# The end of a mixture-of-experts layer: a small expert last but one, its sums between the last one's pieces

## The chip, the cores and the metric

The kernel runs on one core of a Trainium2 chip. The metric is the time of one execution on the device in microseconds (us), as the median of several runs. The engines are TensorE (PE: matmuls), VectorE (DVE), ScalarE (ACT), GpSimd (POOL) and SyncE (SP, which here only issues DMAs). Each works through its own queue in order.

## The reference

One decoder layer on 1024 tokens of width 1024: a mixer (windowed attention and gated linear attention), then a feed-forward part in which a router picks 4 of 32 experts for each token. The change lies in the experts and the final norm:

```
u     = xb @ w_mlp1[e] + b_mlp1[e]                # 1024 -> 2048, even columns gate, odd ones linear
x_glu = jnp.minimum(u[..., ::2], 7.0)
x_lin = jnp.clip(u[..., 1::2], -7.0, 7.0)
a     = x_glu * sigmoid(1.702 * x_glu) * (x_lin + 1)
y     = a @ w_mlp2[e] + b_mlp2[e]                 # summed over a token's 4 experts with its gates
...
x = x + gt2 * rms_norm(y, g_post_ffn)             # the end of the layer, for each token
```

All is float32; the kernel makes each float32 matmul of three float16 ones (high x high, low x high, high x low).

## The kernel before, in words

Experts are ranked by their number of tokens, and rank r has room for `CAPS[r]` tokens (368 down to 60). `ORDER` is the sequence in which the ranks are computed; it alternates large and small ones. Its last four have 244, 80, 152 and 124 tokens; place 18 has 140.

An expert is done in two stages. `up` makes 8 pieces j of 128 gated columns, each from 48 matmuls into PSUM (`pu`). Behind each piece ScalarE makes `gl` (L1127) and `sg` (L1129), VectorE three instructions on `lin` (L1131 to L1133), and GpSimd the float16 pair: a cast to `aTh` (L1134) and the difference `aTl` (L1135). `down` makes the 1024 outputs from 192 matmuls into `pyv`, which ScalarE copies to `yT`. `combine` gives steps: transposes on TensorE, a scaled copy to `yo` on ScalarE (L1173) for each half of a block of 128 tokens, and after the second half an indirect DMA from GpSimd's queue that adds the rows to `yacc` in HBM (L1176).

Weights come as float32 pieces of 1 MB into 7 buffers `st` (L1059, on SP's queue). `split` turns a piece into float16 high parts on ScalarE (`eh`, L172) and low parts on VectorE (`el`, L173), two of each to a megabyte: 16 for an `up`, 8 for a `down`; their buffers hold four pieces of 512 columns ahead of TensorE, which are 16 splits.

The main loop runs `up` of expert i+1 and then `down` of expert i, so that the sequence at the end is up(29), down(28), up(30), down(29), sums of 29, down(30). Steps that are at hand (gathers of expert i+2, sums of i-1) are handed to `up` as `between` and go one by one between its pieces; what is left runs after it. Before the last expert (31, rank 19, 124 tokens) all that is left, the sums of 30, is run at once (`run(left)`).

Then comes the end. The last `up` has no `between`. The rows of `x1d` (the input of the feed-forward part) and of `yacc` (the sum) are loaded for 8 blocks of 128 tokens; each block's row is squared and summed on ScalarE (`square`, L1334), multiplied with the gate row `gfb` on VectorE (L1363), `rms` makes the factors for four blocks at a time, and VectorE scales and adds (L1368) before SP stores the block. The tokens of the last expert, whose sums are not in `yacc`, are gathered by `tokL` (L1342), finished apart (L1383 to L1390), and written over the stored rows by one last indirect DMA (L1391). A run-time loop for experts with more tokens than room follows; it has no rounds here.

The code gives each instruction a program order, and a planner, which has costs of its own, sets each engine's queue from it. `tc.issue_after(ins)` keeps what is traced inside it behind `ins` on that engine. Here the squares of blocks 0 to 3 are held behind `sgs[t - 5]`, the sigmoids of the last `up`'s pieces 3 to 6, and the others behind the activation table's load (`tail`, set 6, which stands behind the last sigmoid).

Of the kernel before, what the change touches and what calls it, by code (L numbers as in the profile page):

```python
# [9 lines left out]
F32 = mybir.dt.float32  # L10
# [3 lines left out]
AF = mybir.ActivationFunctionType  # L14
OP = mybir.AluOpType
# [5 lines left out]
D = 1024  # L21
NT = 8
# [20 lines left out]
ORDER = []  # L43
for _i in range(NE // 4):
    for _r in ((_i + 4) % 8, 15 - (_i + 4) % 8):
        ORDER += [_r, NE - 1 - _r]


@with_exitstack
def layer_kernel(  # L50
# [4 lines left out]
    nc = tc.nc  # L55
    x = x.rearrange("b s d -> (b s) d")
    out = out.rearrange("b s d -> (b s) d")
# [24 lines left out]
    x1d = dram.tile([T, D], F32, name="x1d")  # L82
    yacc = dram.tile([T + DUMP, D], F32, name="yacc")
# [338 lines left out]
    with tc.tile_pool(name="p2", bufs=1) as p2, tc.tile_pool(name="wk", bufs=2) as wk, \  # L422
# [261 lines left out]
        for t in range(NT):  # L684
            tk = slice(t * 128, (t + 1) * 128)
            row = ada_row(t // 2 - 1) if t and t % 2 == 0 else []
# [358 lines left out]
    with tc.tile_pool(name="stB", bufs=7, reuse_waits="tile") as stB, tc.tile_pool(name="sp", bufs=8, reuse_waits="tile") as sp, \  # L1045
# [50 lines left out]
        def run(steps):  # L1096
            while steps:
                steps.pop(0)()

        def up(n, w1e, bc, xT, tag, behind=(), between=(), lead=None, wp=None):  # L1100

            xTh, xTl = xT
            aTh = mo.tile([128, 8, n], F16, name="aTh", tag="aTh" + tag)
# [1 line left out]
            for j in range(8):  # L1105
# [25 lines left out]
                nc.vector.tensor_scalar(lin, pu[1], bc(1, j), bc(2, j), op0=OP.max, op1=OP.min)  # L1131
                nc.vector.scalar_tensor_tensor(lin, lin, bc(3, j), sg, op0=OP.add, op1=OP.mult)  # L1132
                lins.append(nc.vector.scalar_tensor_tensor(lin, gl, LIM * SG, lin, op0=OP.subtract, op1=OP.mult))  # L1133
                nc.gpsimd.tensor_copy(aTh[:, j, :], lin)  # L1134
                lows.append(nc.gpsimd.tensor_tensor(aTl[:, j, :], lin, aTh[:, j, :], op=OP.subtract))  # L1135
                for _ in range((len(between) + 7 - j) // (8 - j)):
                    between.pop(0)()
            return aTh, aTl
# [61 lines left out]
                gi = lambda b: tokL  # L1200
            return gather(CAPS[ORDER[i]], gi, "BS"[i % 2])

        def up_of(i, e, xT, behind=(), between=(), lead=None, wp=None):
            r = ORDER[i]

            def piece_of(j):
                if e[min(j, 1)] is None:
                    with tc.issue_after(loads[-1].ins):
                        e[1] = expert(i, perm1)
                return w1[ds(e[min(j, 1)], 1)]  # L1210

            return up(CAPS[r], piece_of,
                      lambda q, j: bt[:, q, j, r:r + 1], xT, "BS"[i % 2], behind, between, lead, wp)

# [90 lines left out]
        for i in range(NE - 1):  # L1307
# [10 lines left out]
            yTs = down(n, w2[ds(e[1], 1)], aT)  # L1318
            left = combine(n, yTs, si, gc)
            e, aT = en, aTn  # L1320
        run(left)


        i = NE - 1
        r = ORDER[i]
        n = CAPS[r]
        assert n <= 128
        aTh, aTl = up_of(i, e, xT[i][0])
        wps = [w for half in range(2) for w in pieces(w2[ds(e[1], 1)], half)]
        with tc.issue_after(sgs[-1].ins):  # L1330
            tail = act_set(6).ins

        def square(yt, ss, m):
            nc.scalar.activation(junk[:m, 0:yt.shape[-1]], yt, AF.Square, accum_out=ss)  # L1334

        gfb = mo.tile([128, D], F32, name="gfb", tag="xTlB")
        nc.sync.dma_start(gfb, bcast_row(gmod[5:6, :], D))
        junk = mo.tile([128, D], F16, name="junk", tag="xThB")

        rows = [mw.tile([128, D], F32, name=f"row{j}", tag="xg", bufs=4) for j in range(2)]  # L1340
        for row, src in zip(rows, (x1d, yacc)):
            nc.gpsimd.indirect_dma_start(out=row[:n, :], out_offset=None, in_=src,  # L1342
                                         in_offset=bass.IndirectOffsetOnAxis(ap=tokL[:n, 0:1], axis=0))
        xys = []
        for t in range(NT):
            if t < NT - 2:
                st = stB.tile([128, 4, 512], F32, name="st").rearrange("p a n -> p (a n)")
                xys.append((st[:, 0:D], st[:, D:2 * D]))
            elif t < NT - 1:
                xys.append([mw.tile([128, D], F32, name=f"xy{j}", tag="xg", bufs=4) for j in range(2)])  # L1350
            else:
                xys.append([mo.tile([128, D], F32, name=f"xy{j}", tag=f"aT{j}B") for j in "hl"])
        for xy, src, ts in ((0, x1d, range(4)), (1, yacc, range(NT)), (0, x1d, range(4, NT))):
            for t in ts:
                nc.sync.dma_start(xys[t][xy], src[t * 128:(t + 1) * 128, :])
        fs = rt.tile([128, 3, NT + 5], F32, name="fs")
        for t0 in range(0, NT, 4):
            for t in range(t0, t0 + 4):
                yt = xys[t][1]
                with tc.issue_after(sgs[t - 5].ins if t < 4 else tail):  # L1360
                    square(yt, fs[:, 0, t:t + 1], 128)
                with tc.issue_after(lins[min(t - 4, -1)].ins):
                    nc.vector.tensor_tensor(yt, yt, gfb, op=OP.mult)  # L1363
            rms(*[fs[:, j, t0:t0 + 4] for j in range(3)], 128, (tail, lins[-1].ins))
            for t in range(t0, t0 + 4):
                x1, yt = xys[t]
                with tc.issue_after(lins[-1].ins):
                    nc.vector.scalar_tensor_tensor(yt, yt, fs[:, 1, t:t + 1], x1, op0=OP.mult, op1=OP.add)  # L1368
                nc.sync.dma_start(out[t * 128:(t + 1) * 128, :], yt)
        yo = mw.tile([128, D], F32, name="yo")  # L1370
        nc.gpsimd.tensor_copy(si_l[:n], tokI[:n, r:r + 1])
        x1, yt = rows[0][:n], rows[1][:n]
        for half, pool, tag in ((0, psV, "pyv"), (1, psU, "pu")):
            py = [pool.tile([128, 512], F32, name="pyr", tag=tag)[:n, 0:256] for _ in range(2)]
            for k in range(8):
# [115 lines left out]
```

## Time and profile before

| | us |
|---|---|
| median of 3 runs (1977.88 to 1984.84) | 1979.7 |
| the profiled execution, its own time | 1985.62 |
| its span, first to last instruction | 1983.8 |
| TensorE busy in it | 1821.8 |
| VectorE busy | 1553.4 |
| ScalarE busy | 1305.1 |
| GpSimd busy | 981.2 |

Times in the views are microseconds from the start of the span; each instruction has a line of the kernel (L1334), and a tile that it writes and those that it reads (`aTh<-lin`). Matmuls are pipelined, so TensorE's busy time overstates its work.

### The profile page before, as it was taken

What the parts mean: (1) busy time and instruction counts of PE and PEld (TensorE: products, weight loads), DVE (VectorE), ACT (ScalarE), POOL (GpSimd) and SP (SyncE); (2) the same over time, 40 slices, a digit from 0 to 9 for tenths busy, and PEclk for the clock granted to TensorE, in tenths of its full rate; (3) what the DMA queues carried; (4) which work ended last, traced back from release to release, by engine and by line L of the source; (5) the groups of instructions that cost most, each with busy time, mean ns of one, the idle gap of its engine ahead of it and who ended that gap; (6) DMA issues with size and microseconds to landing.
All of it is one profiled execution on the core that took longest, in us unless ns stands there. A gap on an engine that the chain in (4) does not pass through costs nothing. (4 is left out here: it accounts for less than half of the span.)

```text
span 1983.8 us, 55399 instructions
## 1 busy us (share of the span) xinstructions
PE 1821.8 (92%) x22803; PEld 1593.0 (80%) x22803; DVE 1553.4 (78%) x2572; ACT 1305.1 (66%) x2247; POOL 981.2 (49%) x977
## 2 busy tenths in 40 slices
PE   7999999999588999999999999999989999999981
PEld 3456887755387999999999997778878888999971
DVE  6824667656679898998998996679787978989864
ACT  5623455433366878787787885668676868968762
POOL 2204777636636456555574673336443643755430
PEclk9999999989788999999999999999999999999995
DMA  8512333343499999999999997699988989999993
GB/s 280 167 44 75 91 92 98 100 140 128 137 355 321 331 353 320 353 360 329 346 346 361 371 348 268 212 316 327 323 273 292 356 275 338 365 322 327 317 314 129
DMA packets 296246, 525.79 MB, mean 265 GB/s; under 512 B 18672, under 2 KB 79227, under 8 KB 295956
## 3 DMA queue, kind: packets, MB, share of 16 engines
q1 hardware_dynamic: 277810, 476.78, 69.2%
q0 software_dynamic: 16880, 41.21, 8.7%
q8 instruction: 180, 2.95, 0.6%
q10 hardware_dynamic: 1298, 4.21, 0.5%
q14 instruction: 78, 0.64, 0.1%
HBM read 482.37 MB, written 39.76 MB: 263 GB/s over the span
## 5 line engine op out<-in xcount | busy, mean ns | idle before, releaser
L173 DVE SCALAR_TENSOR_TENSOR el<-st,eh 128x1024 f16<-128x1024 f32 x768 | 935.0, 1240 | 91.1 <-ACT eh L172 89.2
L172 ACT ACTIVATE eh<-st 128x1024 f16<-128x1024 f32 x768 | 794.0, 1055 | 237.9 <-PE pu L152 128.7
L151 PE MATMUL pu<-xTh,eh 128*128 128x232 f16 (+31 forms) x4096 | 780.4, 231 | 8.6 <-DVE lin L1131 5.0
L153 PE MATMUL pu<-xTh,el 128*128 128x232 f16 (+31 forms) x4096 | 779.6, 231 | 6.0 <-issue 6.0
L152 PE MATMUL pu<-xTl,eh 128*128 128x232 f16 (+31 forms) x4096 | 779.4, 231 | 2.9 <-issue 2.7
L152 PEld LDWEIGHTS <-eh 128*128 128x128 f16 x6080 | 595.4, 99 | 42.5 <-issue 20.4
L151 PEld LDWEIGHTS <-eh 128*128 128x128 f16 x6080 | 593.1, 98 | 30.1 <-issue 8.1
L153 PEld LDWEIGHTS <-el 128*128 128x128 f16 x6080 | 592.8, 98 | 26.2 <-issue 4.3
L1134 POOL CAST aTh<-lin 128x232 f16<-128x232 f32 (+31 forms) x256 | 298.3, 1165 | 497.3 <-DVE lin L1133 450.2
L151 PE MATMUL pyv<-aTh,eh 128*128 128x232 f16 (+30 forms) x1984 | 374.2, 231 | 9.7 <-ACT yT L1161 7.9
L153 PE MATMUL pyv<-aTh,el 128*128 128x232 f16 (+30 forms) x1984 | 373.7, 230 | 1.2 <-issue 1.2
L152 PE MATMUL pyv<-aTl,eh 128*128 128x232 f16 (+30 forms) x1984 | 373.6, 230 | 0.7 <-issue 0.7
L1135 POOL TENSOR_TENSOR aTl<-lin,aTh 128x232 f16<-128x232 f32 (+31 forms) x256 | 257.8, 1007 | 20.7
L1131 DVE TENSOR_SCALAR lin<-pu,bt 128x232 f32<-128x232 f32 (+31 forms) x256 | 109.8, 429 | 75.5 <-PE pu L153 58.0
L1176 POOL DMA_INDIRECT yacc<-yo,tokI x52 | 95.2, 1832 | 110.4 <-ACT yo L1173 103.8
L1127 ACT ACTIVATE gl<-pu,bt 128x232 f32<-128x232 f32 (+31 forms) x256 | 98.2, 384 | 69.9 <-PE pu L153 40.0
L1132 DVE SCALAR_TENSOR_TENSOR lin<-lin,bt,sg 128x232 f32<-128x232 f32 (+31 forms) x256 | 104.8, 410 | 21.0 <-ACT sg L1129 7.0
L645 POOL TENSOR_TENSOR st<-st,sil 128x512 f32<-128x512 f32 x64 | 68.7, 1074 | 92.6 <-DMA st<-in_w_ada_dram 92.2
L1129 ACT ACTIVATE sg<-gl,c 128x232 f32<-128x232 f32 (+31 forms) x256 | 108.1, 422 | 1.0
L1133 DVE SCALAR_TENSOR_TENSOR lin<-gl,lin 128x232 f32<-128x232 f32 (+31 forms) x256 | 82.9, 324 | 4.3
L1089 POOL DMA_INDIRECT xg<-h2d,gatI x50 | 71.7, 1434 | 24.4 <-PE pxh L1081 12.3
L1081 PE MATMUL pxh<-identh,xg 128*128 128x128 f16 (+27 forms) x848 | 55.7, 206 | 23.9 <-DVE xTl L1083 11.4
(408 smaller groups left out, 2495.5 us busy)
## 6 DMA issues: line engine op xcount, KB each, us to landing
st<-in_w_mlp_dram SPq DMA_DIRECT2D x384, 1024.0 KB
st<-in_w_ada_dram SPq DMA_DIRECT2D x64, 256.0 KB
xt<-in_x_dram SPq DMA_DIRECT2D x16, 512.0 KB
st<-in_w_ada_dram SPq DMA_DIRECT2D x16, 512.0 KB
st<-in_w_in_dram SPq DMA_DIRECT2D x7, 1024.0 KB
x1d<-xt SPq DMA_DIRECT2D x8, 512.0 KB
h2d<-h2s SPq DMA_DIRECT2D x8, 512.0 KB
yacc<-yi ACTq DMA_DIRECT2D x8, 512.0 KB
```

The costliest lines, as they stand in the source:

```text
L151: nc.tensor.matmul(ps, sh, mh, start=first, stop=False)
L152: nc.tensor.matmul(ps, sh, ml, start=False, stop=False)
L153: return nc.tensor.matmul(ps, sl, mh, start=False, stop=last)
L172: return (nc.scalar.activation(dh, src, AF.Copy, scale=SW), nc.vector.scalar_tensor_tensor(dl, src, SW, dh, op0=OP.mult, op1=OP.subtract))
L173: nc.vector.scalar_tensor_tensor(dl, src, SW, dh, op0=OP.mult, op1=OP.subtract))
L1127: nc.scalar.activation(gl, pu[0], AF.Relu, scale=-SG, bias=bc(0, j))
L1129: sgs.append(nc.scalar.activation(sg, gl, AF.Sigmoid, scale=-1.702 * INV / SG, bias=c7))
L1131: nc.vector.tensor_scalar(lin, pu[1], bc(1, j), bc(2, j), op0=OP.max, op1=OP.min)
L1132: nc.vector.scalar_tensor_tensor(lin, lin, bc(3, j), sg, op0=OP.add, op1=OP.mult)
L1134: nc.gpsimd.tensor_copy(aTh[:, j, :], lin)
L1135: lows.append(nc.gpsimd.tensor_tensor(aTl[:, j, :], lin, aTh[:, j, :], op=OP.subtract))
L1176: end["dma"] = nc.gpsimd.indirect_dma_start(out=yacc, out_offset=bass.IndirectOffsetOnAxis(ap=si(b)[:m, :], axis=0), in_=yo[:m, :], in_off ...
```

## The change

`ORDER` is altered in three places: rank 15 (140 tokens) goes from place 18 to place 29, rank 12 (152) from place 30 to place 18, rank 28 (80) from place 29 to place 30. The last four then have 244, 140, 80 and 124 tokens. `run(left)` ahead of the last `up` is taken out, and the sums of expert 30 (one block of 80, two steps) are handed to it as `between`. That `up` is called with `pool=False`: its casts are made by ScalarE and its differences by VectorE. Block 7 takes the place of block 1 in the sequence; blocks are taken as (0, 7, 1, 2) and (3, 4, 5, 6). Loads: all eight of `x1d`, then all eight of `yacc`, then the two gathers of the last expert's rows. Squares and gate products of blocks 0 and 7 are held behind the last but one sigmoid and the last but one gated product, those of the other six behind the last ones.

```diff
+ORDER[ORDER.index(15)], ORDER[-3], ORDER[-2] = 12, 15, 28
...
-                nc.gpsimd.tensor_copy(aTh[:, j, :], lin)
-                lows.append(nc.gpsimd.tensor_tensor(aTl[:, j, :], lin, aTh[:, j, :], op=OP.subtract))
+                if pool:
+                    nc.gpsimd.tensor_copy(aTh[:, j, :], lin)
+                else:
+                    nc.scalar.activation(aTh[:, j, :], lin, AF.Copy)
+                eng = nc.gpsimd if pool else nc.vector
+                lows.append(eng.tensor_tensor(aTl[:, j, :], lin, aTh[:, j, :], op=OP.subtract))
...
-        run(left)
...
-        aTh, aTl = up_of(i, e, xT[i][0])
+        aTh, aTl = up_of(i, e, xT[i][0], (), left, pool=False)
...
+        def rows_of(tok, m, src, **place):
+            row = mw.tile([128, D], F32, name="row", **place)
+            nc.gpsimd.indirect_dma_start(out=row[:m, :], out_offset=None, in_=src,
+                                         in_offset=bass.IndirectOffsetOnAxis(ap=tok[:m, 0:1], axis=0))
+            return row
...
-        rows = [mw.tile([128, D], F32, name=f"row{j}", tag="xg", bufs=4) for j in range(2)]
-        for row, src in zip(rows, (x1d, yacc)):
-            nc.gpsimd.indirect_dma_start(out=row[:n, :], out_offset=None, in_=src,
-                                         in_offset=bass.IndirectOffsetOnAxis(ap=tokL[:n, 0:1], axis=0))
         xys = []
         for t in range(NT):
-            if t < NT - 2:
+            if t == 0:
+                xys.append([mw.tile([128, D], F32, name=f"xy{j}", tag="xg", bufs=4) for j in range(2)])
+            elif t < NT - 1:
                 st = stB.tile([128, 4, 512], F32, name="st").rearrange("p a n -> p (a n)")
                 xys.append((st[:, 0:D], st[:, D:2 * D]))
-            elif t < NT - 1:
-                xys.append([mw.tile([128, D], F32, name=f"xy{j}", tag="xg", bufs=4) for j in range(2)])
             else:
                 xys.append([mo.tile([128, D], F32, name=f"xy{j}", tag=f"aT{j}B") for j in "hl"])
-        for xy, src, ts in ((0, x1d, range(4)), (1, yacc, range(NT)), (0, x1d, range(4, NT))):
-            for t in ts:
+        for xy, src in enumerate((x1d, yacc)):
+            for t in (0, NT - 1, *range(1, NT - 1)):
                 nc.sync.dma_start(xys[t][xy], src[t * 128:(t + 1) * 128, :])
+        x1l, ytl = [rows_of(tokL, n, src, tag="xg", bufs=4) for src in (x1d, yacc)]
         fs = rt.tile([128, 3, NT + 5], F32, name="fs")
-        for t0 in range(0, NT, 4):
-            for t in range(t0, t0 + 4):
+        for ts, pin in (((0, 7, 1, 2), -2), ((3, 4, 5, 6), -1)):
+            j0 = 4 * (pin == -1)
+            for j, t in enumerate(ts):
                 yt = xys[t][1]
-                with tc.issue_after(sgs[t - 5].ins if t < 4 else tail):
-                    square(yt, fs[:, 0, t:t + 1], 128)
-                with tc.issue_after(lins[min(t - 4, -1)].ins):
+                at = min(pin + j // 2, -1)
+                with tc.issue_after(sgs[at].ins):
+                    square(yt, fs[:, 0, j0 + j:j0 + j + 1], 128)
+                with tc.issue_after(lins[at].ins):
                     nc.vector.tensor_tensor(yt, yt, gfb, op=OP.mult)
```

## Rows read from the trace of the kernel before

**Rows 1.** The page's first part: busy time, share, instructions.
```profile
PE 1821.8 (92%) x22803; PEld 1593.0 (80%) x22803; DVE 1553.4 (78%) x2572; ACT 1305.1 (66%) x2247; POOL 981.2 (49%) x977
```

**Rows 2.** Stretches of the end: length, each engine's busy time (instructions), clock, DMA.
```profile
1902.60:1922.70 20.10, 20.10 (x370) 20.10 (x368) 15.25 (x25) 15.48 (x27) 7.80 (x11) 1.00 0.92 289
1922.70:1936.30 13.60, 5.96 (x42) 4.62 (x40) 6.23 (x13) 4.46 (x9) 5.03 (x7) 0.75 0.99 285
...
1967.90:1983.80 15.90, 0.00 (x0) 0.00 (x0) 0.00 (x0) 0.00 (x0) 1.35 (x1) 0.50 0.12 34
```

**Rows 3.** GpSimd's timeline: start, length, instruction [idle before, what ended it].
```profile
1904.50 1.40 POOL L1176 DMA_INDIRECT yacc<-yo,tokI  x1 [0.55 <-ACT yo L1173]
1913.87 1.33 POOL L1342 DMA_INDIRECT row<-yacc,tokL  x1 [7.97 <-DMA yacc<-yo,tokI]
...
1967.92 1.35 POOL L1391 DMA_INDIRECT out_dram<-row,tokL  x1 [29.84 <-SPq L1408]
```

**Rows 4.** ScalarE's timeline in the last up-projection.
```profile
1917.87 1.06 ACT L1334 ACTIVATE junk<-st 128x1024 f16<-128x1024 f32 x1 [2.59 <-DMA st<-yacc]
1918.83 0.19 ACT L1334 ACTIVATION_READ_ACCUMULATOR junk<-st 128x1 f32 x1
...
1928.24 1.06 ACT L1334 ACTIVATE junk<-st 128x1024 f16<-128x1024 f32 x1 [5.55 <-DMA st<-yacc]
...
1933.59 1.06 ACT L1334 ACTIVATE junk<-st 128x1024 f16<-128x1024 f32 x1 [3.52 <-DMA st<-yacc]
...
1934.64 0.34 ACT L1127 ACTIVATE gl<-pu,bt 128x124 f32<-128x124 f32 x1
```

**Rows 5.** VectorE's timeline in the last up-projection and at the end.
```profile
1916.04 0.41 DVE L1131 TENSOR_SCALAR lin<-pu,bt 128x124 f32<-128x124 f32 x1 [3.14 <-POOL aTl L1135]
...
1936.00 0.29 DVE L1133 SCALAR_TENSOR_TENSOR lin<-gl,lin 128x124 f32<-128x124 f32 x1
...
1954.96 1.28 DVE L1368 SCALAR_TENSOR_TENSOR xyl<-xyl,fs,xyh 128x1024 f32<-128x1024 f32 x1
```

**Rows 6.** SP's timeline: issues of loads and stores, neighbours merged (xN).
```profile
1913.60 0.80 SPq L1355 DMA_DIRECT2D st<-yacc  x2
...
1945.84 1.53 SPq L1369 DMA_DIRECT2D out_dram<-st  x2
...
1956.92 0.99 SPq L1369 DMA_DIRECT2D out_dram<-xyl  x1
```

**Rows 7.** Stretches: up(140), down(140), up(80), up(152), down(80), sums of 29; columns as above.
```profile
1324.90:1352.50 27.60, 27.60 (x439) 27.31 (x438) 21.23 (x30) 22.97 (x36) 15.06 (x14) 1.00 0.87 247
1388.80:1400.80 12.00, 12.00 (x201) 11.96 (x199) 11.69 (x18) 8.51 (x13) 9.50 (x8) 1.00 1.05 375
1806.60:1825.10 18.50, 16.77 (x429) 16.36 (x427) 17.69 (x30) 18.32 (x32) 8.86 (x11) 1.00 1.03 347
1846.50:1874.50 28.00, 28.00 (x421) 27.95 (x420) 25.14 (x36) 23.81 (x36) 15.44 (x14) 1.00 0.94 291
1874.40:1882.50 8.10, 7.25 (x197) 7.15 (x195) 8.06 (x11) 7.30 (x12) 5.75 (x5) 1.00 0.93 307
1882.50:1887.30 4.80, 1.44 (x17) 1.24 (x16) 3.67 (x4) 3.17 (x5) 1.03 (x1) 1.00 1.09 356
```

**Rows 8.** VectorE's groups from 1899 on: count, busy, mean ns, idle before.
```profile
L173 DVE SCALAR_TENSOR_TENSOR el<-st,eh 128x1024 f16<-128x1024 f32 x11 | 13.6, 1240 | 3.1 <-ACT eh L172 3.1
...
L1363 DVE TENSOR_TENSOR st<-st,gfb 128x1024 f32<-128x1024 f32 x6 | 7.3, 1219 | 0.5 <-ACT junk L1334 0.5
L1131 DVE TENSOR_SCALAR lin<-pu,bt 128x124 f32<-128x124 f32 x8 | 3.2, 402 | 10.1 <-ACT gl L1127 6.6 <-POOL aTl L1135 3.5
L1132 DVE SCALAR_TENSOR_TENSOR lin<-lin,bt,sg 128x124 f32<-128x124 f32 x8 | 2.9, 363 | 0.3
L1133 DVE SCALAR_TENSOR_TENSOR lin<-gl,lin 128x124 f32<-128x124 f32 x8 | 2.3, 283 | 0.2
```

**Rows 9.** ScalarE's timeline in the up-projection of 152 tokens.
```profile
1854.64 0.69 ACT L1173 ACTIVATE yo<-pxy,gcol 128x512 f32<-128x512 f32 x1
```

More of the change, by code (lines that the diff above doesn't have):

```diff
@@ L1098, in run, with up @@
                 steps.pop(0)()
-        def up(n, w1e, bc, xT, tag, behind=(), between=(), lead=None, wp=None):
+        def up(n, w1e, bc, xT, tag, behind=(), between=(), lead=None, wp=None, pool=True):
             xTh, xTl = xT
@@ L1201, in fetch, with up_of @@
             return gather(CAPS[ORDER[i]], gi, "BS"[i % 2])
-        def up_of(i, e, xT, behind=(), between=(), lead=None, wp=None):
+        def up_of(i, e, xT, behind=(), between=(), lead=None, wp=None, pool=True):
             r = ORDER[i]
@@ L1212, in up_of @@
             return up(CAPS[r], piece_of,
-                      lambda q, j: bt[:, q, j, r:r + 1], xT, "BS"[i % 2], behind, between, lead, wp)
+                      lambda q, j: bt[:, q, j, r:r + 1], xT, "BS"[i % 2], behind, between, lead, wp, pool)
         e = [expert(0, perm), None]
@@ L1363, in layer_kernel @@
                     nc.vector.tensor_tensor(yt, yt, gfb, op=OP.mult)
[L1364 to L1369, printed above, removed]
+            rms(*[fs[:, j, j0:j0 + 4] for j in range(3)], 128, (tail, lins[-1].ins))
@@ L1370, in layer_kernel @@
+            with tc.issue_after(lins[-1].ins):
+                for j, t in enumerate(ts):
+                    x1, yt = xys[t]
+                    nc.vector.scalar_tensor_tensor(yt, yt, fs[:, 1, j0 + j:j0 + j + 1], x1, op0=OP.mult, op1=OP.add)
+                    nc.sync.dma_start(out[t * 128:(t + 1) * 128, :], yt)
         yo = mw.tile([128, D], F32, name="yo")
         nc.gpsimd.tensor_copy(si_l[:n], tokI[:n, r:r + 1])
-        x1, yt = rows[0][:n], rows[1][:n]
+        x1, yt = x1l[:n], ytl[:n]
```

## The prediction

> **What bounds the kernel now.** I read the page first: TensorE and VectorE are both busy most of the span [rows 1], so the body is a balance, and an edit there pays only where one of them waits. Then the table of stretches of the end [rows 2]. The last expert's up-projection ends near 1922.7 us. In the next 13.6 us TensorE is busy for 5.96 us and its granted clock falls from 1.00 to 0.75 in the mean (a mix of the 2.4 and the 1.2 GHz level): something starves it while it should be doing the last down-projection.
>
> The timelines say what starves it. GpSimd issues the second sum of the last but one expert into `yacc` at 1904.50 and then the gather of `yacc` rows at 1913.87, which waited 7.97 us for that sum to land [rows 3]. It is an in-order queue: the casts and differences of the last expert (L1134, L1135) stand behind that gather, and VectorE waits 3.14 us for one of them at 1916.04 [rows 5]. ScalarE has the squares of the output rows (L1334) between the last expert's activations. They wait for rows of `yacc`, 5.55 us at 1928.24 and 3.52 us at 1933.59, and so the last `gl` comes only at 1934.64 [rows 4]. The last gated product (L1133) starts at 1936.00 and ends at 1936.29 [rows 5]: 13.6 us after TensorE had its sum ready. That is the wait that ends last in this stage, and it is on the path: from 1936.3 VectorE works with hardly a pause until the last output row is scaled at 1956.24 (19.95 us), the last output store is issued at 1956.92 [rows 6], the final scatter waits for all stores and starts at 1967.92 [rows 3], 11.0 us later, and the run ends 15.9 us after that [rows 2]. So the end of the kernel is the time of the last gated product plus 47.5 us, and the change must move that product or shorten what follows.
>
> **The change, part by part.** (a) *The order.* The sequence 244, 80, 152, 124 at the end becomes 244, 140, 80, 124, and 152 takes the place of 140 at place 18. TensorE's matmuls are the same in all; what changes is where it waits. An up-projection of 140 tokens takes 27.6 us, one of 80 takes 18.5 us (VectorE is busy for 17.69 us of it), one of 152 takes 28.0 us [rows 7]. Down-projections take 12.0 us (140) and 8.1 us (80) [rows 7]. The up-projection of the last but one therefore begins at 1846.5 + (27.6 − 18.5) = 1855.6 us, plus at place 18 0.4 us up and 0.8 us down (12.0 × 152/140 = 13.0, 1.0 more, of which I take 0.8), so 1856.8. Then 18.5 (80 up) + 12.0 (140 down) + 4.8 (sums that run at once, as before [rows 7]) + 8.1 (80 down) = 43.4: the last up-projection begins at 1900.2. It has 384 matmuls; 370 took 20.1 us [rows 2], so 20.9 us, and I allow 0.6 us for the eight transposes that now stand between its pieces: it ends at 1921.7, against 1922.7. The order itself gives 1.0 us there.
>
> VectorE can be later than that. From 1856.8 it has 40 weight differences to make (56 for the projections left, less 16 for the four pieces that the buffers hold ahead) at 1.24 us, and 16 groups of gating products at 0.40 + 0.36 + 0.28 us [rows 8]; 49.6 + 16.6 = 66.2 us, 1923.0. Both answers agree within 1.3 us.
>
> (b) *Casts and differences on ScalarE and VectorE.* This removes 8 casts and 8 differences from GpSimd and with them the 3.14 us wait. No row shows the cast on ScalarE; the nearest is `gl` of the same width, 0.34 us [rows 4], from below it is nothing if ScalarE waits anyway; I take 0.34, 8 × 0.34 = 2.7 us on ScalarE, hidden as long as it waits for rows. The difference on VectorE is nearest to L1133, 0.28 us [rows 8]: 2.3 us, which I add: 1925.3, with the price zero as the lower bound (1923.0) if the differences fall into VectorE's waits. Half of it gives 1924.2 for the last gated product without any other wait.
>
> (c) *Sums between pieces.* The sum of 80 tokens has one block, not two, and its halves come after pieces 0 and 1. In the up-projection of 152 its like did this: the second half's ScalarE copy starts at 1854.64 [rows 9], 8.1 us after the start at 1846.5, with pieces of 28.0/8 = 3.5 us. Here they are 2.7 us, so the copy is at 1900.2 + 8.1 − 1.6 = 1906.7, the sum is issued at about 1907.6, later than the 1904.50 of before. It landed 9.4 us after its issue [rows 3], which gives 1917.0, 3.5 us later than before. This is the edit's cost: SP's loads of `yacc` and GpSimd's gather both stand behind it. What was queued behind that gather on GpSimd was the casts; now nothing is. The first row of `yacc` was in use 4.3 us after its issue (1913.60 [rows 6] to 1917.87 [rows 4]), which gives 1921.3 here.
>
> The Trainium skill, in "DMA: Bandwidth & Descriptors", section "Anatomy of one DMA — SWDGE (gpsimd) path", fits one such transfer by 2.0 us plus its bytes at 436 GB/s; for 80 rows of 4 KB that is 2.8 us, an estimate from that page. The trace disagrees with its 9.4 us under load. By the page the rows would be in use at 1914.7 and the next part's 1.8 us would vanish.
>
> (d) *Squares and products at the end.* Six of eight squares no longer stand ahead of any `gl`. Those of rows 0 and 7 stand behind the seventh sigmoid and so ahead of the last `gl`: two squares and their products. With the rows at 1921.3 and, say, 1922.5, and 1.25 us each (1.06 + 0.19), the squares end at 1923.8, a cast of 0.34 us comes between, and the last `gl` starts at about 1924.2. From that start to the end of the last product it took 1.65 us before (1934.64 to 1936.29), so it ends at 1925.9, say 1926.0. That is 1.8 us later than without them, and 10.3 us ahead of 1936.3. TensorE's last down-projection then runs without the long pauses and off the path, and its clock's fall no longer matters.
>
> Behind it VectorE has six products of 1.22 us [rows 8] left where it had five: 19.95 + 1.22 = 21.2 us, to 1947.2 (bounds: 20 if the cover is better, 23.6 if none of the eight is done ahead). ScalarE's six squares, 7.5 us, run beside it. The eight loads of `x1d` now all come ahead of `yacc`, into the time before the sum lands, so less has to move afterwards: 8 rows of 0.5 MB and the gather, 4.5 MB, at the 285 GB/s of that stretch [rows 2] take 15.8 us, to about 1934 with 1 us for the last landing; VectorE reaches the second four at about 1935. So the loads are just hidden; if they are 5 us later they end last.
>
> (e) *Stores.* Before, first store to scatter was 1945.84 [rows 6] to 1967.92, 22.1 us for 4.5 MB. The first four rows now leave some 8 us ahead of the second four, so 2.5 MB are left behind 1942, at the same 0.2 MB/us 12.5 us, and from 1947.2 that is 7 to 8 us instead of 11.7 after the last scaled row (bounds 4.3, one transfer's landing, and 11.7). I take 8: the scatter at 1955.2.
>
> **The sum.** 1955.2 + 15.9 = 1971.1 us of span, 12.7 less than 1983.8. The profiled execution took 1985.6 us, so 1972.9 by its own time; it stands 5.9 us above the median of the three runs, 1979.7, and on that I forecast 1979.7 − 12.7 = 1967.0.
>
> **The rivals.** *1, rows late:* the sum is issued later, the `x1d` loads stand ahead of `yacc` on SP, and row 6's load needs a weight buffer that is free only after the next to last split. If the two rows come at 1930 and not 1922, each us delays the last `gl` by one: gain about 5, time 1975. For it: the sum's 9.4 us, and the squares of the third and fourth row ran 14.6 and 20.0 us after the loads of `yacc` began. Against it: four `x1d` loads shared that time, and the 3.14 us stall that held the splits up is gone.
>
> *2, light experts together:* 80 and 124 now follow each other with VectorE as the bound; if the four pieces ahead are not all there at 1856.8, up to 7.0 us (one piece's four differences and two groups) are added. Gain 5.7, time 1974. For it: 17.69 us busy of 18.5 for an expert of 80. Against it: 28 us of 140 and 21 of down-projection before it let VectorE catch up.
>
> *3, slower:* the same place as rival 1, with the price large: the last weight differences are placed behind the gating products, the sixth `x1d` load waits for them, the `yacc` loads behind it, and the two squares hold the last `gl`. By the terms above the scatter comes 1926.0 − 1922 + 21.2 + 8 = 33.2 us behind the landing of rows 0 and 7, so the kernel is slower than before once they land after 1934.7, and by more than 0.3% after 1940.6; at 1942 the time is 1987.
>
> *4, better:* if the sums land as fast as a plain load and the stores leave as they come, the last product is at 1922.5 and the scatter 4.3 us behind the last row: 1922.5 + 20 + 4.3 = 1946.8, a gain of 21, time 1959.
>
> **How the numbers follow.** Forecast 0.55 (its own range 1962 to 1973), rival 1 0.17, rival 2 0.10, rival 3 0.10, rival 4 0.08. A change under 0.3% (5.9 us), about what this kernel's measurement can tell from none, counts as same. Faster: 0.55 + 0.08 + half of rivals 1 and 2, less a little for their tails, 0.74; same 0.15; slower 0.11. The range runs from rival 4 to beyond rivals 1 and 2: 1959 to 1980.
>
> **What would show it.** Right: no GpSimd row L1134 in the last expert; the sum inside it, issued near 1908; the last L1133 near 1926; TensorE at full clock to the end of the last down-projection; first store near 1934; last store near 1948; scatter near 1955. Wrong: a long wait of a square ahead of the last `gl`, or the last up-projection beginning well behind 1900.

## The result, and the profile after

| | median us (runs) | ratio to before, 95% interval |
|---|---|---|
| before | 1979.7 (21) | |
| after | 1991.56 (21) | 1.0055 [1.0035, 1.0076] |

The change costs 0.55%, about 11 us. Forecast were 1967.0 in a range of 1959 to 1980, with a chance of 0.11 for slower. The profiled execution of after took 1989.26 us with a span of 1987.1, only 3.3 us longer than that of before: the profiled execution of before lies 5.9 us above its kernel's median, this one 2.3 us below. So the traces show where time goes, and the medians how much.

The table of stretches of after, with the columns of [rows 2, 7]: up of 80, down of 140, the pause behind it, down of 80, the last up, from its end to the last gated product, the rest of TensorE's work, and the last scatter to the end.

```profile
1848.10:1864.70 16.60, 16.60 (x421) 16.55 (x419) 14.91 (x25) 16.52 (x28) 9.82 (x9) 1.00 0.79 231
1864.70:1880.60 15.90, 12.24 (x195) 11.86 (x193) 15.90 (x22) 12.49 (x19) 7.86 (x11) 1.00 0.96 322
1880.60:1883.80 3.20, 0.85 (x7) 0.56 (x6) 2.14 (x3) 1.35 (x2) 0.00 (x0) 0.95 0.97 334
1883.80:1896.20 12.40, 10.48 (x207) 9.61 (x206) 7.88 (x8) 10.82 (x16) 2.97 (x2) 0.74 1.03 350
1896.20:1918.40 22.20, 21.98 (x394) 21.79 (x392) 20.67 (x34) 17.19 (x32) 4.75 (x3) 1.00 1.02 348
1918.40:1937.30 18.90, 5.70 (x42) 4.64 (x40) 5.54 (x12) 5.81 (x12) 0.00 (x0) 0.66 0.93 245
1937.30:1948.10 10.80, 9.20 (x54) 8.55 (x54) 8.58 (x15) 8.59 (x23) 0.00 (x0) 0.65 0.12 47
...
1970.90:1987.10 16.20, 0.00 (x0) 0.00 (x0) 0.00 (x0) 0.00 (x0) 1.34 (x1) 0.50 0.12 33
```

The starving stretch behind the last up-projection, 13.6 us in [rows 2], is now 18.9 us, with the same 42 matmuls in it. ScalarE's timeline there (square is L1340 now, the cast L1139, `gl` L1129):

```profile
1919.35 0.35 ACT L1129 ACTIVATE gl<-pu,bt 128x124 f32<-128x124 f32 x1
...
1932.02 1.06 ACT L1340 ACTIVATE junk<-xy 128x1024 f16<-128x1024 f32 x1 [11.89 <-DMA xy<-yacc]
...
1933.08 0.29 ACT L1139 ACTIVATE aTh<-lin 128x124 f16<-128x124 f32 x1
1933.73 1.06 ACT L1340 ACTIVATE junk<-xyl 128x1024 f16<-128x1024 f32 x1 [0.37 <-DMA xyl<-yacc]
...
1934.79 0.34 ACT L1129 ACTIVATE gl<-pu,bt 128x124 f32<-128x124 f32 x1
```

One wait of 11.89 us has taken the place of the two of 5.55 and 3.52 us in [rows 4]: the sign that the prediction named for being wrong. The square waits for block 0 of `yacc`; behind it stand, on the same engine, the cast of the seventh piece and the last `gl`, which comes at 1934.79. GpSimd's and SP's timelines say that the row was not asked for late:

```profile
1906.95 1.49 POOL L1182 DMA_INDIRECT yacc<-yo,tokI  x1 [14.65 <-DMA xyh<-x1d]
1908.75 1.79 POOL L1344 DMA_INDIRECT row<-x1d,tokL  x1 [0.30 <-issue]
1915.55 1.46 POOL L1344 DMA_INDIRECT row<-yacc,tokL  x1 [5.01 <-DMA yacc<-yo,tokI]
1970.91 1.34 POOL L1401 DMA_INDIRECT out_dram<-row,tokL  x1 [53.90 <-SPq L1418]
```
```profile
1914.66 0.32 SPq L1362 DMA_DIRECT2D xy<-yacc  x1
1915.03 0.42 SPq L1362 DMA_DIRECT2D xyl<-yacc  x1
1915.50 15.12 SPq L1362 DMA_DIRECT2D st<-yacc  x6
...
1951.29 0.35 SPq L1379 DMA_DIRECT2D out_dram<-xy  x1
```

The sum was issued at 1906.95 and the load of block 0 left at 1914.66, both near the forecast. The last `x1d` load had left at 1913.95, and what SP waited for last ahead of block 0 was the sum (0.2 us). The row was in use at 1932.02, 17.4 us after its load was issued, where I had reckoned with 4.3. In those 17 us two gathers of the last expert's 124 rows were under way (L1344). That of `x1d` was issued at 1908.75, but in the trace its first packet began at 1914.34, behind the sum's and just ahead of block 0's load; the last row of the two ended near 1936. Before, only the gather of `yacc` was in this stretch [rows 3], while that of `x1d` had been issued at 1786.59:

```profile
1786.59 1.32 POOL L1342 DMA_INDIRECT row<-x1d,tokL  x1 [0.30 <-issue]
```

VectorE's timeline in after shows the rest of the tail:

```profile
1936.96 0.29 DVE L1135 SCALAR_TENSOR_TENSOR lin<-gl,lin 128x124 f32<-128x124 f32 x1
...
1945.09 1.22 DVE L1373 TENSOR_TENSOR st<-st,gfb 128x1024 f32<-128x1024 f32 x1
1947.76 0.48 DVE L1393 SCALAR_TENSOR_TENSOR row<-pyr,gcolL,row 124x256 f32<-124x256 f32 x1 [1.46 <-PE pyr L155]
...
1949.98 1.28 DVE L1378 SCALAR_TENSOR_TENSOR xy<-xy,fs,xy 128x1024 f32<-128x1024 f32 x1
...
1956.13 4.87 DVE L1378 SCALAR_TENSOR_TENSOR st<-st,fs 128x1024 f32<-128x1024 f32 x4
```

The last gated product ends at 1937.25 and not near 1926. All eight gate products (to 1946.3) and the evictions of the last expert, which wait for TensorE, stand ahead of the first scaled row.

What two gathers do to a load is seen in the DMA view: busy tenths of the 16 engines in 40 equal slices, GB/s in each, and queue 0, which is GpSimd's. First after, 1915 to 1935, and then the run a1_gather128 (below), in which only the two gathers differ, 128 rows for 124, over the same time:

```profile
DMA  7699999999999999999999999999989998899755
GB/s 164 254 360 344 270 262 254 262 262 246 254 246 246 262 205 221 246 230 295 279 262 221 238 279 238 189 238 303 295 213 352 352 221 205 254 328 287 205 148 188
...
q0 software_dynamic: 671, 0.94, 20.2%
```
```profile
DMA  9599998999999999999999999999733322000000
GB/s 320 221 360 410 418 410 352 377 311 410 385 385 418 377 410 377 410 426 401 418 418 418 434 418 401 401 410 410 295 131 156 131 98 98 33 25 8 0 0 0
...
q0 software_dynamic: 211, 0.75, 9.5%
```

Both show all engines "busy", but together they move about 250 GB/s in the one and 410 in the other. The busy digit only says that packets are out; the GB/s line is the one to read. After has more than three times as many packets on queue 0, but the rows go in packets of 4 KB in both; 443 of the 671 are of 4 bytes.

The packets of the loads themselves (queue 1) say more. From 1917 to 1929 584 of 4 KB began in after, and 580 of them took over 175 ns (median 256 ns); in a1 it was 16 of 1039 (median 159 ns). In before, with one gather, all 319 from 1920 to 1926 took over 175 ns. So a gather of 124 rows slows nearly every packet of the loads, not only the share that would stand beside it on a few engines; by what, no run here shows.

The last scatter, with nothing beside it, shows a transfer of 124 rows by itself. After (124 rows, 1971 to 1987) and the run a4_cap128 (128 rows, 1957 to 1966.2):

```profile
DMA  0000342324030322223211100000000000000000
...
DMA packets 515, 0.53 MB, mean 33 GB/s; under 512 B 388, under 2 KB 388, under 8 KB 512
...
q0 software_dynamic: 512, 0.51, 12.1%
```
```profile
DMA  0100001999994100000000000000000000000000
...
DMA packets 147, 0.55 MB, mean 60 GB/s; under 512 B 16, under 2 KB 16, under 8 KB 144
...
q0 software_dynamic: 144, 0.52, 14.0%
```

Half a megabyte takes some 8 us at two to four tenths in the one, in 512 packets, and some 1.5 us at nine tenths in the other, in 144. Of these 124 and 128 are the rows, the rest are of 4 bytes. In the stretch 1973 to 1981 of after the DMA share is 0.23, close to 4 of 16. In the trace the rows' packets overlap 3.4 deep in the mean there (four for most of the time, five at most) and take 226 ns each; in a4 they overlap 14 deep (16 for most of the time, 18 at most) and take 160 ns.

```profile
1973.00:1981.00 8.00, 0.00 (x0) 0.00 (x0) 0.00 (x0) 0.00 (x0) 0.00 (x0) 0.50 0.23 63
```

The Trainium skill, "DMA: Bandwidth & Descriptors", section "Why a DMA increments its semaphore by 16 and not by 1", has a rule that fits: a DMA is spread over the largest number of engines, up to 16, that divides the sizes of its slowest dimension (it leaves some direct copies from GpSimd's queue out). By it 124 rows go to 4 engines, 127 to 1, 128 to 16. It agrees with these indirect DMAs: a share of 0.23 here for 124 rows, nine tenths for 128, and one row's packet at a time for 127 (a6_gather127, below). I had not used it; the prediction has no charge for the gather that the change moves.

### The profile page after: what moved, and what is told of

The parts are those of the page before. It is cut to its first block, busy times and chain, and to the rows that moved or that the text cites. A ratio compares the mean times of both kernels' runs of the same rounds, so it can differ in the third digit from the quotient of the medians.

```text
span 1987.1 us, 55391 instructions
## 1 busy us (share of the span) xinstructions
PE 1824.0 (92%) x22803; PEld 1593.4 (80%) x22803; DVE 1557.7 (78%) x2580; ACT 1307.1 (66%) x2255; POOL 977.8 (49%) x961
## 5 line engine op out<-in xcount | busy, mean ns | idle before, releaser
L154 PEld LDWEIGHTS <-eh 128*128 128x128 f16 x6080 | 595.4, 99 | 42.2 <-issue 20.1
L1137 POOL CAST aTh<-lin 128x232 f16<-128x232 f32 (+30 forms) x248 | 285.4, 1151 | 475.2 <-DVE lin L1135 454.8
L1141 POOL TENSOR_TENSOR aTl<-lin,aTh 128x232 f16<-128x232 f32 (+30 forms) x248 | 264.7, 1067 | 20.0
L1129 ACT ACTIVATE gl<-pu,bt 128x232 f32<-128x232 f32 (+31 forms) x256 | 97.9, 383 | 66.2 <-PE pu L155 39.7
L1179 ACT ACTIVATE yo<-pxy,gcol 128x512 f32<-128x512 f32 (+26 forms) x104 | 70.6, 679 | 4.9 <-DMA yacc<-yo,tokI 4.6
```

The source lines that it names most:

```text
L154: nc.tensor.matmul(ps, sh, ml, start=False, stop=False)
L1129: nc.scalar.activation(gl, pu[0], AF.Relu, scale=-SG, bias=bc(0, j))
L1141: lows.append(eng.tensor_tensor(aTl[:, j, :], lin, aTh[:, j, :], op=OP.subtract))
```

## The experiments

Two theories of the 17.4 us. **Rows:** a transfer of 124 rows uses 4 of the 16 engines, and the loads, which are spread over all 16, are held up on those four; the change moved a second such transfer to where a load's latency is kernel time. **Backlog:** the loads of `x1d` that now stand ahead of those of `yacc`, 4 MB, take that time whatever the gathers do. A third question is whether the order, or the casts, lose time by themselves. Medians and ratios are against runs of before on the same chip (medians 1980.8 to 1982.8); "first row" is what block 0's square waits for. Where the intervals of two kernels overlap, a difference of their medians is not clear by itself.

**a1_gather128.** Both gathers of 128 rows (the four more are not used):
```diff
-        x1l, ytl = [rows_of(tokL, n, src, tag="xg", bufs=4) for src in (x1d, yacc)]
+        x1l, ytl = [rows_of(tokL, 128, src, tag="xg", bufs=4) for src in (x1d, yacc)]
```


> The changed kernel with one number altered: the two gathers of the last expert's rows read 128 rows of tokL and not 124 (the last four are padding that repeats a token; only 124 are used). Split theory: a gather of 124 rows runs on 4 of the 16 DMA engines, beside which the loads of x1d and yacc wait on those four, and this made rows 0 and 7 land 17 us after their issue; with 128 rows it runs on 16, the gathers are through in 3 to 6 us, rows 0 and 7 land by 1921, the last gated product comes near 1924 and not 1937.3, and the time is 10 to 14 us under that of the changed kernel: 1978 to 1982. Backlog theory: the loads of yacc are late because eight loads of x1d and both gathers move 5 MB just ahead of them; 4 more rows change nothing, time 1990 to 1993, the first square still waits over 9 us.

Measured: 1981.92 us, 1.0011 [0.9996, 1.0026]. Four more rows per gather take some 9 us off the kernel (0.44%, and the intervals do not overlap) and leave it level with before. The wait is 3.62 us for 11.89, the last `gl` 2.4 us behind it:
```profile
1924.08 1.06 ACT L1340 ACTIVATE junk<-xy 128x1024 f16<-128x1024 f32 x1 [3.62 <-DMA xy<-yacc]
...
1926.48 0.34 ACT L1129 ACTIVATE gl<-pu,bt 128x124 f32<-128x124 f32 x1
```
The backlog is unchanged here, so it is not the cause of the 8 us that went. What is left, 9.1 us from issue (1914.99) to use, is more than expected (rows by 1921) and may be the backlog's share; no run here takes the backlog away.

**a6_gather127.** The dose: both gathers of 127 rows.
```diff
-        x1l, ytl = [rows_of(tokL, n, src, tag="xg", bufs=4) for src in (x1d, yacc)]
+        x1l, ytl = [rows_of(tokL, 127, src, tag="xg", bufs=4) for src in (x1d, yacc)]
```


> The changed kernel with the two gathers reading 127 rows. Split theory, with the largest divisor of the row count up to 16 as the number of engines: 127 is prime, so each gather has one engine; 31 packets on an engine took about 18 us beside the loads, 127 take 60 us or more, the loads wait for that engine: 2020 to 2060. If it is only that 124 is not the full 128, or that packets go out in sixteenths rounded up: like 128, 1976 to 1990. Backlog theory: like the changed kernel, 1985 to 1997.

Measured once: 2001.24 us, span 1999.1. The sign and the reason held, the size was too high. At most one row's packet of queue 0 is out at a time from 1917 to 1929. The loads beside it suffer less than with four engines taken (342 GB/s in these 12 us), though queue 0 has 1575 packets of 4 bytes there, for 272 in after; so those are not what slows the loads:
```profile
1929.49 1.06 ACT L1340 ACTIVATE junk<-xy 128x1024 f16<-128x1024 f32 x1 [9.02 <-DMA xy<-yacc]
```
but the gathers themselves drag on, when nearly all else has landed, one or two rows at a time and 54 GB/s, and the last expert's evictions wait 13.46 us for the gathered rows, until 1953.40:
```profile
1933.00:1949.00 16.00, 8.36 (x56) 7.45 (x54) 4.83 (x7) 7.50 (x16) 0.00 (x0) 0.71 0.13 54
```

**a2_early_gather.** The gather of `x1d` goes ahead of the loads, as before the change:
```diff
+        x1l = rows_of(tokL, n, x1d, tag="xg", bufs=4)
...
-        x1l, ytl = [rows_of(tokL, n, src, tag="xg", bufs=4) for src in (x1d, yacc)]
+        ytl = rows_of(tokL, n, yacc, tag="xg", bufs=4)
```


> The changed kernel with the gather of x1d rows traced ahead of the loads, as in the kernel before; the gather of yacc rows stays. Split theory: one of the two slow gathers is gone from the end; row 0 is in front of the other one and lands by 1920, row 7 in part behind it, and the last gated product comes 5 to 12 us earlier: 1980 to 1987. Backlog theory: 0.5 MB of 9 MB less, under 2 us: 1989.5 to 1992.

Measured: 1985.07, 1.0034 [1.0010, 1.0059]. The first two squares wait 2.86 and 2.63 us:
```profile
1918.59 1.06 ACT L1340 ACTIVATE junk<-xy 128x1024 f16<-128x1024 f32 x1 [2.86 <-DMA xy<-yacc]
...
1922.57 1.06 ACT L1340 ACTIVATE junk<-xyl 128x1024 f16<-128x1024 f32 x1 [2.63 <-DMA xyl<-yacc]
```
The last gated product ends at 1926.08, 35.2 us after the start of the last up, for 41.25 in after. So the gather that the change moved is the larger part of the wait. With that gather out of the way the kernel gains 6.5 us on after by the medians and 0.21% by the ratios, which is not clear by itself.

**a3_no_early_square.** No square or product ahead of the last `gl` (blocks 0 and 7 join the others):
```diff
-        for ts, pin in (((0, 7, 1, 2), -2), ((3, 4, 5, 6), -1)):
-            j0 = 4 * (pin == -1)
+        for ts, pin in (((0, 7, 1, 2), -1), ((3, 4, 5, 6), -1)):
+            j0 = 4 * (ts[0] == 3)
```


> The changed kernel with the squares and products of rows 0 and 7 behind the last sigmoid and the last gated product, too. Both load theories leave the rows landing at 1932 to 1941. Pin theory (the cost is that two squares stand ahead of the last activation): the last gated product comes near 1922, TensorE ends near 1938, but the eight squares and products wait for rows until about 1942, so the end gains what the evictions and the last expert's row no longer put between: 4 to 10 us, 1981 to 1988. If the rows alone set the end and the pin costs nothing: 1990 to 1993.

Measured: 1987.14, 1.0027 [1.0009, 1.0046]; the median is 4.4 us below that of after, not clear by itself. ScalarE's timeline shows why not more:
```profile
1927.07 0.35 ACT L1129 ACTIVATE gl<-pu,bt 128x124 f32<-128x124 f32 x1
...
1938.08 1.06 ACT L1340 ACTIVATE junk<-xy 128x1024 f16<-128x1024 f32 x1 [8.61 <-DMA xy<-yacc]
```
With the last up 7 us later in this execution the last `gl` no longer waits, TensorE is done at 1935.7, and then the rows are waited for all the same: the wait has moved behind the `gl`, and the rows are the bound.

**a4_cap128** and **b4_before_cap128.** The capacity itself is 128, so that the last scatter and every other DMA of that expert has 128 rows; in the changed kernel and in the one before:
```diff
-        136, 132, 128, 124, 120, 112, 108, 104, 100, 96, 92, 84, 80, 72, 64, 60]
+        136, 132, 128, 128, 120, 112, 108, 104, 100, 96, 92, 84, 80, 72, 64, 60]
```


> The changed kernel with room for 128 tokens and not 124 in the last expert, so that its gathers, its store to yld and the last scatter all have 128 rows. Split theory: what the 128-row gathers give (10 to 14 us), the last scatter and the run's end 16.2 us after its issue shrink by 4 to 6 us, the stores by 1 to 3, less 1 us for matmuls 3% wider: 1970 to 1978. Backlog theory: 1 us more, 1991 to 1994.

> The kernel before with room for 128 tokens and not 124 in the last expert. Split theory: its gather of yacc rows, its store to yld and its last scatter ran on 4 engines too. The two waits of 5.6 and 3.5 us ahead of the third and fourth square go for the most part, the last gated product comes 6 to 9 us earlier, the stores end 3 to 5 us sooner after it and the run ends 9 us and not 15.9 after the last scatter's issue: 15 to 20 us under before, 1960 to 1966, and so below the changed kernel with 128 (1971). Backlog theory: the squares wait for eight loads of yacc that come with four of x1d; only the last scatter gains: 1973 to 1977.

Measured: 1971.48, 0.9953 [0.9928, 0.9978], and 1963.13, 0.9899 [0.9863, 0.9934]. The scatter to the end takes 9.2 us in both, for 15.9 in [rows 2]; that is 6.7 of the 17.7 us between the medians of before and b4. In the kernel before the waits of 5.55 and 3.52 us of [rows 4] shrink to 1.8 and 0.86: so the stall of ScalarE that the change set out to remove was largely the gather of 124 rows. On this clean base the change loses some 0.5% (the intervals overlap by 0.06%).

**b1_order_only** and **o1_last_two.** The kernel before with the new order alone, and with 152, 80 for 80, 152 at the end alone (140 stays at place 18):
```diff
+ORDER[ORDER.index(15)], ORDER[-3], ORDER[-2] = 12, 15, 28
```
```diff
+ORDER[-3], ORDER[-2] = 12, 28
```


> The kernel before with the new order alone. My reckoning: the last up-projection ends 1.0 us sooner and one scatter of 80 rows takes the place of two, so the rows of yacc come 1 to 3 us sooner: 1976 to 1980. Light experts together: VectorE and the weights become the bound ahead of the last expert, up to 6 us: 1983 to 1987.

> The kernel before with only the two experts ahead of the last exchanged (244, 152, 80, 124), place 18 left at 140. If the order's cost (1993 for the order alone against 1981) stands at place 18, where the stage of 140 or 152 and its neighbour took 75.8 to 76.2 us in the old order and 78.1 to 80.6 in the new: 1980 to 1985. If it stands at the end, where the down-projection of the heavier neighbour waits for weights, TensorE pauses ahead of the sums and its clock falls: 1987 to 1994.

Measured: 1993.32, 1.0057 [1.0036, 1.0078], and 1989.54, 1.0033 [1.0008, 1.0059]. The order alone loses as much as the whole change, and more than either range of what was expected of b1; o1 came as expected of a cost at the end. From the start of the up at place 18 to that at place 20 it takes 78.1 us in b1 and 78.2 in after, against 75.8 before; the eight traces of the new order have 78.1 to 80.6 there, the nine others 75.0 to 76.9. From the start of the last but two up to the start of the last one it is 96.3 (b1) and 98.9 (o1), against 93.4 before; but b4 and c4, which do the same work as before up to there, have 95.9 and 95.2, so that only o1 stands out.

**a9_old_order.** The change without its order (the sums that go between the pieces are then those of 152 tokens, four steps):
```diff
-ORDER[ORDER.index(15)], ORDER[-3], ORDER[-2] = 12, 15, 28
```


> The changed kernel with the old order; its last but one has 152 tokens, so four steps go between pieces 0 to 3. If the order costs what the run with it alone shows (6 to 12 us): 1980 to 1987, less than that by the sum's issue, which comes up to 5 us later and holds the rows of blocks 0 and 7. If the order costs nothing: 1992 to 1997, by those 5 us.

Measured: 1984.31, 1.0021 [0.9989, 1.0053], by the medians 7.2 us less than after, not clear by itself. Its last sum is issued at 1912.50, 5.6 us later than in after, and its first row still waits 10.23 us.

**a8_pool_casts** and **c4_cap128_no_pool.** The casts alone: after with casts and differences back on GpSimd, and b4 with them on ScalarE and VectorE (it also has the change's `if pool:` lines in `up`):
```diff
-        aTh, aTl = up_of(i, e, xT[i][0], (), left, pool=False)
+        aTh, aTl = up_of(i, e, xT[i][0], (), left)
```
```diff
-        aTh, aTl = up_of(i, e, xT[i][0])
+        aTh, aTl = up_of(i, e, xT[i][0], pool=False)
```


> The changed kernel with the last expert's casts and differences on GpSimd as before; order, sums between the pieces, squares as changed. What the casts on ScalarE cost: one of them (piece 6) stood behind the blocked square for 11.9 us; without that TensorE's last down-projection and the evictions end about 2 us sooner; against it the casts of pieces 2 to 4 stand behind the gather of yacc rows on GpSimd (5 us). The last gated product still waits for rows 0 and 7, so 1988 to 1993. If GpSimd's stall counts for more than I think: over 1995.

> The kernel before with room for 128 tokens in the last expert and its casts and differences on ScalarE and VectorE (the second part of the change alone, on the better base). VectorE's wait for GpSimd behind the gather of yacc rows goes (3 us), the casts stand behind squares that now wait 1 to 2 us: 1958 to 1963; if the casts on ScalarE cost more than GpSimd's stall did: 1964 to 1968.

Measured: 1993.05, 1.0048 [1.0022, 1.0073], which is no difference from after, and 1960.26, 0.9876 [0.9843, 0.9909], 2.9 us less than b4 and inside its interval.

**a10_old_order_128** and **a11_old_order_128_late.** The change without its order and with 128; a11 also holds squares of blocks 0 and 7 behind the last sigmoid, as a3:
```diff
-ORDER[ORDER.index(15)], ORDER[-3], ORDER[-2] = 12, 15, 28
...
-        136, 132, 128, 124, 120, 112, 108, 104, 100, 96, 92, 84, 80, 72, 64, 60]
+        136, 132, 128, 128, 120, 112, 108, 104, 100, 96, 92, 84, 80, 72, 64, 60]
```


> The changed kernel with the old order and room for 128 in the last expert: what is left of the change are the sums between the pieces (four steps), the casts on ScalarE and VectorE, and the moved loads, squares and products, on a base without gathers over four engines. The kernel before on that base took 1963.1. If these parts are worth what was forecast for them once rows land quickly (10 us): 1952 to 1957. If the later sum and the two squares ahead of the last activation eat it: 1961 to 1967.

> The same with the squares and products of blocks 0 and 7 behind the last activations. If the pin is what is left of the loss: 3 to 6 us under the run beside it. If the rows alone set the end: the same within 2 us.

Measured: 1967.4, 0.9937 [0.9912, 0.9962], and 1963.06, 0.9918 [0.9895, 0.9940]. With good rows, without the order and without the early squares the rest of the change (sums between pieces, casts, products at the end) is just level with b4's 1963.13. The 4.3 us between the two are of the sign and size expected of the pin, but their intervals overlap.

**d1_other_caps** and **e1_best.** The kernel before with the other capacities whose last block has an awkward number of rows (244 = 128 + 116, 204 = 128 + 76, 92) made 248, 208 and 96, and 124 made 128; e1 adds the casts of c4:
```diff
-CAPS = [368, 292, 260, 244, 232, 216, 204, 192, 184, 176, 168, 160, 152, 148, 144, 140,
-        136, 132, 128, 124, 120, 112, 108, 104, 100, 96, 92, 84, 80, 72, 64, 60]
+CAPS = [368, 292, 260, 248, 232, 216, 208, 192, 184, 176, 168, 160, 152, 148, 144, 140,
+        136, 132, 128, 128, 120, 112, 108, 104, 100, 96, 96, 84, 80, 72, 64, 60]
```


> The kernel before with 128 for 124 and also 248 for 244, 208 for 204 and 96 for 92, so that no block of over 4 rows has to go over four engines (116, 76 and 92 rows did). Their matmuls get 1 us longer for each, 2.9 us. If such gathers and sums held up the weights beside them as they did the rows at the end: 1956 to 1961. If there the weights are far enough ahead: 1963 to 1967.

> The kernel before with 128, 248, 208 and 96 tokens of room (1957.0) and the casts and differences of the last expert on ScalarE and VectorE (2.9 us better on the base with 128 alone): 1953 to 1957 if the two add up, 1957 to 1960 if they do not.

Measured: 1957.0, 0.9861 [0.9828, 0.9894], and 1953.75, 0.9864 [0.9821, 0.9907]. Twelve more rows of work make the kernel some 6 us faster than b4 by the medians (the intervals overlap), in the range expected. From the start of the last but two up to the start of the last one it takes 91.0 us in d1 and 91.5 in e1, for 95.9 in b4 and 93.4 in before. The casts of e1 add nothing to d1 by the ratios and 3.3 us by the medians. Both beat both kernels; e1 is 1.4% below before, and its median 1.9% below that of after.

## Why the prediction was wrong

Set from the start of the last up, the forecast and the trace of after add up as follows (us):

| | forecast | after |
|---|---|---|
| last up starts to last gated product ends | 25.8 | 41.25 |
| to the last scaled row's end | 21.2 | 23.75 |
| to the scatter | 8.0 | 9.9 |
| to the end | 15.9 | 16.2 |
| sum | 70.9 | 91.1 |

The start itself was forecast at 1900.2 and came at 1896.0; in the traces of before and b4, which are the same up to there, the last but two up begins 4.6 us apart, so that part is no gain of the change.

**(c), the step that failed.** "The first row of `yacc` was in use 4.3 us after its issue (…), which gives 1921.3 here." It was 17.4 us, 13.1 more, and that is most of the 15.45 us of the first line. The 4.3 us came from a load issued just ahead of the gather [rows 3, 6], so it had left before the gather's packets came; [rows 4] held the price with the gather in flight, 5.55 and 3.52 us of waiting for blocks 2 and 3, and I put that down to the amount of data at 285 GB/s, which was itself the sign of the disturbance: 410 GB/s with 128 rows (a1). I then moved a second gather there and did not count it at all: the 4.5 MB of (d) are eight rows and one gather. That the number of rows in the gathers is the cause is shown by a1, in time and in the trace, and a6 agrees in its trace; that the pair takes more than one is shown by the waits of a2, not clearly by its time.

**(c), the issue.** The sum left 10.95 us after the start of the last up, where 7.4 were forecast, and landed 7.7 us later and not 9.4: net 1.8 us late. The delay is ScalarE's: its copies for the sum stand right behind `gl` of pieces 0 and 1 (1901.91 and 1906.01), and the first `gl` comes 5.65 us after the start of the up, behind three splits. Whether those splits were late for want of weights or stood badly in the queue I did not test.

**(d).** Two squares ahead of the last `gl` were priced at 1.8 us because their rows would be there. They make the rows' latency the kernel's: with the pin gone a3 gains 4.4 us on after and a11 4.3 on a10, of one sign, neither clear by itself. "TensorE's last down-projection then runs without the long pauses and off the path" fell with it: it ended at 1948.05 with a mean clock of 0.65 in its last 10.8 us (a mix of the 2.4 and the 1.2 GHz level), and the evictions that wait for it stand ahead of the first scaled row. The VectorE tail came out at the bound that I gave for no cover (23.6).

**(a).** The order was to gain 1.0 us and loses by itself 0.57% [0.36, 0.78], some 7 to 15 us. The 1.0 us did not follow even from its own terms. In before the last up starts at 1900.04, its first 18 matmuls between the transposes of the sums, so a start at 1900.2 gained nothing; the stretch of 20.1 us in [rows 2] begins 2.6 us into that up, which takes 22.65 us in all (22.35 in after, where I had 21.5):
```profile
1900.04 0.22 PE L151 MATMUL pu<-xTh,eh 128*128 128x124 f16 x1
```
Of the loss the traces show 2.3 us at places 18 to 20, where I had 1.2, and up to 3 us at the end (b1 against the 93.4 of before; against b4 and c4 it is 0.4 and 1.1). In after the start of the last up comes 92.9 us behind that of the last but two, close to my 92.4, but by errors that cancel: the up of 140 and the down of 244 took 45.0 (49.0 forecast), the up of 80 16.6 (18.5), the down of 140 15.9 (12.0), the pause 3.2 (4.8), and the down of 80 12.4 (8.1), at a mean granted clock of 0.74 after that pause, again a mix of the two levels. In the down of 140 VectorE is busy for all of the 15.9 us and TensorE for 12.24:
```profile
1873.79 8.22 DVE L175 SCALAR_TENSOR_TENSOR el<-st,eh 128x1024 f16<-128x1024 f32 x7
```
```profile
1881.98 1.06 ACT L174 ACTIVATE eh<-st 128x1024 f16<-128x1024 f32 x1 [3.58 <-DMA st<-in_w_mlp_dram]
```
VectorE has no pause of over 0.12 us from 1850.68 to 1882.01. SP's loads of weights wait for it to free a buffer (29.7 us in all from 1845 to 1900, 8.0 at most), and ScalarE's split then waits 3.58 us for weights. So rival 2, two light experts together with VectorE as the bound, was there in its way. With the sums run ahead of the last up, as in b1, the pause that they leave (3.4 us) comes on top. The stages found sum to 3 to 5 us; where the rest of the order's loss is stays open.

**(b).** Right in size or nearly: nothing to be measured in after (a8, 1.5 us), 2.9 us by the medians in c4 against b4; in e1 against d1 3.3 us by the medians and nothing by the ratios (0.9864 and 0.9861). None is clear by itself.

**(e).** The last scaled row to the scatter was 9.9 us, within the bounds of 4.3 and 11.7. That four rows would leave early was wrong: first store at 1951.29, not near 1934.

**The rivals.** Rivals 1 and 3 had the place, ScalarE held by rows of `yacc` ahead of the last `gl`, and rival 3 the sign. Their reasons were others, four `x1d` loads ahead in SP's queue or a weight buffer that comes late. A late `x1d` load as in rival 3 was there (the last one left 4.25 us behind the one before it), but behind it the loads of `yacc` still waited for the sum; they left at 1914.66, and with the same loads ahead a1 is level with before. Rival 3's condition, loss from a landing after 1934.7 with a last up that starts at 1900.2, is a landing at 34.5 us behind that start; here it was 36.0. So rival 3's price of a late row was right, with another reason for the lateness.

**What the loss consists of.** Taken out one at a time, the rows are worth 0.44% (1.0055 less 1.0011) and the order 0.34% (a9) to 0.57% (b1, where it comes alone); both together are more than the 0.55%. Of these a1's and b1's are clear of the noise, a9's is not. Whether they overlap or the other parts give some of it back, no run here separates; the order alone with 128 rows was not run. On the base with 128 rows the other parts give nothing back: a11 is level with b4.

## What to carry to other kernels

Look at the number of rows of a DMA before its bytes: a scatter of 124 rows went at 63 GB/s by itself, and beside two gathers of 124 rows the engines moved 250 GB/s in all; with 128 rows it was some 410 in both, and rounding four capacities up was worth 1.4%, more than any reordering tried here. A load's latency is only good for a forecast if it was read with the same traffic in flight that the change will put there. An instruction that waits for memory is a risk ahead of the last activation that TensorE waits for, even if its data "should" be there: it cost some 4 us by the medians in two pairs of runs.

## What the runs showed of the hardware that was not expected

- The scatter of 124 rows takes 512 packets, 388 of them of 4 bytes, and some 8 us alone, that of 128 rows 144 packets and some 1.5 us; scatter to end 16.2 and 9.2 us.
- The view's DMA share stays near 1.0 while the bytes moved fall from some 410 to 250 GB/s. Beside two gathers of 124 rows 580 of 584 packets of the loads took over 175 ns, beside two of 128 rows 16 of 1039.
- 127 rows disturb the loads less (9.02 us wait for 11.89) and take longer themselves: one row's packet at a time from 1917 to 1929, and with both gathers out 54 GB/s at the end.
